# Ninety-four further index pairs in the list that edits an instruction order (hybrid attention step, one core)

## The chip, the cores and the metric

The kernel runs on one core of a Trainium2 chip, as one program. The metric is the device time of one execution in microseconds; lower is better. Where several runs are given, the median is meant.

## The reference, cut to what matters

One layer is computed for a prompt of 1024 rows and, with the same weights, for a sample group of 32 rows that also reads caches of 512 keys. Eight heads use a banded softmax attention with a relative-position bias (A), eight use stick-breaking attention (B).

```python
def in_proj(h, g_pre, w_in):
    u = rmsnorm(h, g_pre) @ w_in            # 1024 -> 4096: qa ka va ga qb kb vb gb
...
def band_attention(q, k, v, q_pos, k_pos, bias_table):
    s = jnp.einsum('bqhd,bkhd->bhqk', q, k).astype(jnp.float32) * ATTN_SCALE
    s = s + bias_table[:, rel].astype(jnp.float32)[None]
    s = jnp.where(ok[None, None], s, NEG_INF)      # own 64-frame chunk and 8 before it
    return jnp.einsum('bhqk,bkhd->bqhd', jax.nn.softmax(s, axis=-1), v)
...
def stick_breaking(q, k, v, q_pos, k_pos):
    log_beta = jax.nn.log_sigmoid(z)
    log_1m = jnp.where(causal, jax.nn.log_sigmoid(-z), 0.0)
    after = lax.cumsum(log_1m, axis=3, reverse=True) - log_1m
    w = jnp.where(causal, jnp.exp(log_beta + after), 0.0).astype(v.dtype)
...
def finish(h, oa, ga, ob, gb, w_out, g_post, p, w_ple, w_ple_gate):
    y = jnp.concatenate([oa * jax.nn.silu(ga), ob * jax.nn.silu(gb)], axis=-1) @ w_out
    h = h + rmsnorm(y, g_post)
    return h + jax.nn.sigmoid(h @ w_ple_gate) * (p @ w_ple)
```

## The kernel before, in words

**Stages.** Rows are normalised and transposed in nine tiles of 128 (`scale_x`, `turn_x`, tiles `sq`, `ptx`, `hnh`, `hnl`). The projection walks over 32 column groups of 128 (`col_steps`, accumulators `mm_qA`, `mm_kB` and so on), each in three chunks of 352 rows and 24 matmuls, since every FP32 operand is split into a high and a low half. Between them are woven the attention units: for each pair of heads and each of eight row blocks a score step (`scores`, PSUM tiles `SA`, `SB`, three banks in turn), a step that turns the weights (`weights_t`) and a value step (`values`, `PVA`, `PVB`). The later blocks of A (4 to 7) and B (4 to 6) turn their weights by way of DRAM: VectorE transposes a tile `om` in squares, a DMA stores it to `swapA` or `swapB`, and a second DMA brings it back into `be`; ScalarE then makes the high half `wTh` and VectorE the low half `wTl`. The working tiles `om`, `be`, `wTh` and `wTl` are cut from four ring buffers; a new piece waits until all readers of the old piece are done. The sample's attention loads its cached keys (`Kcs`) and values (`Vcs`) into the `be` ring. The output projection and the gate follow (o0P to g3P in the trace), with weights split and summed beforehand (`sum_dro`, `sum_drg`).

**Order.** Nothing is issued as the Python code calls it. `Recorder` collects some 9,400 operations with their dependencies, `plan` schedules them by a list of costs and due times, over and over, and `settle` then edits the winning list by hand-written pairs. `emit` issues the edited list; every engine, and SP for all DMAs, runs its share of the list in that order. A pair `(i, j)` takes the operation at place `i` and puts it at place `j`. Operations between them that it needs are taken along; the others stand behind it:

```python
for i, j in MOVES:
    x = ops[i]
    need, engines, ahead, behind = set(x.after), {x.eng}, [], []
    for o in reversed(ops[j:i]):
        if o in need or (o.eng in engines and o.eng != x.eng):
            ahead.append(o)
            need |= o.after
        ...
        else:
            behind.append(o)
    ops[j:i + 1] = ahead[::-1] + [x] + behind[::-1]
```

The pairs are applied one after the other, each to the list that the last one left, so a pair may undo part of an earlier one. All instructions stand at line 543, in `emit`; they are told apart by their tiles' names, in which buffer numbers are left out.

Of the kernel before, what the change touches and what calls it, by code (L numbers as in the profile page):

```python
# [59 lines left out]
    (6179, 6177), (4602, 4574), (5279, 5267), (1443, 1442), (847, 825), (5478, 5470), (4425, 4416), (3015, 2987), (6270, 6253), (2916, 2915),  # L60
    (2473, 2471), (5581, 5579), (6257, 6245), (5280, 5277), (4266, 4259), (240, 163), (4268, 4262), (5961, 5948), (5470, 5465), (6233, 6217),
    (4269, 4264), (4644, 4633), (1050, 1024), (4531, 4505), (2270, 2244), (1328, 1327), (4499, 4478), (2906, 2862), (1042, 997), (164, 155),
    (2916, 2915), (4633, 4620), (6698, 6684), (2245, 2244), (6511, 6457), (9153, 9149),
)
PASSES, SPREAD = 42, 400

# [1912 lines left out]
```

## Time and profile before

| | |
|---|---|
| median of three runs | 769.75 us (769.07 to 770.1) |
| time of the profiled execution | 769.5 us |
| its span, first to last instruction | 767.7 us, so 1.8 us lie around it |
| granted clock | 0.998 |
| TensorE (PE) busy | 757.9 us, 4422 matmuls |
| VectorE (DVE), ScalarE (ACT), GpSimd (POOL) busy | 589.1, 489.8, 459.7 us |
| DMA | 182.24 MB, 237 GB/s on average, all issued from SP |

Times in the trace count from the span's start. A row of the timeline gives start, duration, engine, operation, the tiles written and read, and in brackets how long the engine was idle before it and what ended that. In the view of waits, a row gives the engine that waited, for whom, the total, how many times and the longest. In the chain that ended last, a DMA's duration runs from its issue to its landing.

### The profile page before, as it was taken

Reading aid. Unit: us, or ns where it says so; the run is one execution under the profiler, and the core shown is the slowest. Engines: PE = TensorE matmul, PEld = TensorE weight load, DVE = VectorE, ACT = ScalarE, POOL = GpSimd, SP = SyncE. Lnnn points to the kernel's source line nnn. Section 1 sums busy time; section 2 is a strip of 40 time slices with the busy share of each in tenths; the row PEclk is TensorE's granted clock in tenths of the full one; section 3 lists DMA queues with packets and bytes.
Section 4 is the critical chain, followed back from the end, with each engine's and each line's share of the span. In section 5 each row is a group of like instructions: output and inputs, shape, how many; then the busy total and the mean of one; then the engine's idle time right before and its main releaser. Section 6 shows DMA issues by size and latency. Waiting matters only on the chain.

```text
span 767.7 us, 13670 instructions
## 1 busy us (share of the span) xinstructions
PE 757.9 (99%) x4422; PEld 701.4 (91%) x4422; DVE 589.1 (77%) x1025; ACT 489.8 (64%) x995; POOL 459.7 (60%) x525
## 2 busy tenths in 40 slices
PE   8999999999999999999999999999999999999997
PEld 7999999999999999999999999999998877888786
DVE  6816889898799888987898787974573578587565
ACT  6736686567685658775668685633447867774551
POOL 6614637874354546656883335787453769898443
PEclk9999999999999999999999999999999999999999
DMA  8519998878876559999779789877688859879754
GB/s 275 173 38 278 286 316 273 240 221 262 229 234 211 146 158 282 266 280 285 198 239 275 176 235 280 241 226 220 198 275 253 280 158 336 273 250 333 278 182 137
DMA packets 184825, 182.24 MB, mean 237 GB/s; under 512 B 42177, under 2 KB 139497, under 8 KB 184754
## 3 DMA queue, kind: packets, MB, share of 16 engines
q1 hardware_dynamic: 184754, 181.37, 77.6%
q8 instruction: 35, 0.57, 0.3%
q14 instruction: 36, 0.29, 0.1%
HBM read 107.62 MB, written 65.30 MB: 225 GB/s over the span
## 4 chain that ended last, share of the span: by engine, by line
PE 93%; DMA 4%; ACT 1%; DVE 1%; SPq 0%; issue 0%; ACTq 0%
PE mm_qA L543 6%; PE mm_vA L543 6%; PE mm_gB L543 6%; PE mm_kB L543 6%; PE mm_qB L543 6%; PE mm_kA L543 6%; PE mm_gA L543 5%; PE PVB L543 4%; PE mm_vB L543 4%; PE SB L543 4%; PE SA L543 4%; PE ple L543 3%; PE PVA L543 3%; PE g1P L543 3%; PE o3P L543 3%; PE o1P L543 3%
## 5 line engine op out<-in xcount | busy, mean ns | idle before, releaser
L543 POOL TENSOR_TENSOR be<-om 128x128 f32<-128x128 f32 (+7 forms) x64 | 78.0, 1224 | 55.3 <-DVE om L543 23.1
L543 DVE TENSOR_TENSOR_SCAN om<-om,SB 128x384 f32<-128x384 f32 (+5 forms) x96 | 94.4, 999 | 9.1 <-ACT om L543 8.1
L543 DVE TENSOR_TENSOR wTl<-be,wTh 128x640 fp32r<-128x640 f32 (+2 forms) x56 | 64.4, 1153 | 11.2 <-ACT wTh L543 11.1
L543 ACT ACTIVATE om<-SB 128x384 f32<-128x384 f32 (+5 forms) x96 | 44.7, 492 | 26.7 <-PE SB L543 15.1
L543 ACT CAST wTh<-be 128x640 fp32r<-128x640 f32 (+2 forms) x56 | 43.1, 774 | 19.6 <-DMA be<-swapA 12.9
L543 ACT ACTIVATE be<-om,statA 128x640 f32<-128x640 f32 (+3 forms) x64 | 46.5, 731 | 13.7 <-DVE wTl L543 6.3
L543 DVE STREAM_TRANSPOSE om<-be 128x640 f32<-128x640 f32 (+2 forms) x56 | 49.5, 890 | 4.2 <-ACT be L543 2.5
L543 POOL TENSOR_TENSOR gB<-gB,gB 128x256 f32<-128x256 f32 x32 | 25.9, 830 | 16.6 <-DMA gB<-in_w_ple_gate_dram 9.9
L543 DVE CUSTOM_DVE_ANT_0 om<-SA,biasA 128x320 f32<-128x320 f32 (+3 forms) x64 | 29.8, 483 | 7.1 <-PE SA L543 5.6
L543 ACT CAST wTh<-ptwB 128x512 fp32r<-128x512 f32 (+3 forms) x48 | 22.0, 483 | 18.6 <-PE ptwB L543 13.7
L543 PE MATMUL SB<-kdB,LB 128*128 128x384 f32 (+5 forms) x96 | 32.6, 345 | 1.1 <-DVE om L543 1.1
L543 PE MATMUL SB<-klB,LB 128*128 128x384 f32 (+5 forms) x96 | 32.9, 347 | 0.0
L543 DVE TENSOR_TENSOR wTl<-ptwB,wTh 128x512 fp32r<-128x512 f32 (+3 forms) x48 | 25.4, 542 | 6.6 <-PE PVB L543 3.9
L543 POOL TENSOR_TENSOR sggA<-sggA,oggA 128x352 f32<-128x352 f32 x24 | 26.2, 1097 | 6.1 <-DVE sggA L543 5.7
L543 PE MATMUL SA<-kdA,LA 128*128 128x320 f32 (+2 forms) x96 | 29.5, 317 | 0.1
L543 PE MATMUL SA<-klA,LA 128*128 128x320 f32 (+2 forms) x96 | 29.5, 319 | 0.0
L543 POOL TENSOR_TENSOR oB<-oB,oB 128x256 f32<-128x256 f32 x32 | 25.5, 822 | 5.0 <-DMA oB<-in_w_out_dram 5.0
L543 DVE TENSOR_TENSOR SB<-SB,maskb 128x128 f32<-128x128 f32 x64 | 18.1, 291 | 12.5 <-PE SB L543 12.1
L543 POOL TENSOR_TENSOR klB<-stkB,kdB 64x1024 fp32r<-64x1024 f32 x8 | 19.3, 2415 | 11.5 <-ACT kdB L543 10.7
L543 POOL TENSOR_TENSOR klA<-stkA,kdA 64x1024 fp32r<-64x1024 f32 x8 | 19.5, 2437 | 8.0 <-ACT kdA L543 7.8
L543 POOL TENSOR_TENSOR h<-h,x 128x512 f32<-128x512 f32 (+1 forms) x18 | 23.1, 1297 | 1.5 <-DVE h L543 1.4
L543 PE MATMUL ptwB<-ident,be 128*128 128x128 f32 x144 | 21.6, 273 | 0.0
(683 smaller groups left out, 2586.8 us busy)
## 6 DMA issues: line engine op xcount, KB each, us to landing
swapA<-om SPq DMA_DIRECT2D x32, 320.0 KB
be<-swapA SPq DMA_DIRECT2D x32, 320.0 KB
oB<-in_w_out_dram SPq DMA_DIRECT2D x16, 256.0 KB
sum_dro<-oB SPq DMA_DIRECT2D x16, 256.0 KB
gB<-in_w_ple_gate_dram SPq DMA_DIRECT2D x16, 256.0 KB
sum_drg<-gB SPq DMA_DIRECT2D x16, 256.0 KB
x<-in_x_prompt_dram SPq DMA_DIRECT2D x16, 256.0 KB
turned<-hs SPq DMA_DIRECT2D x16, 256.0 KB
```

Source lines behind the costliest of these rows:

```text
L543: getattr(getattr(tc.nc, o.what[0]), o.what[1])(*args, **kw)
```

## The change: 94 pairs more

The change appends 94 pairs to `MOVES`; nothing else differs. No operation is added or taken away, and no size, buffer or dependency changes.

```diff
-    (2916, 2915), (4633, 4620), (6698, 6684), (2245, 2244), (6511, 6457), (9153, 9149),
+    (2916, 2915), (4633, 4620), (6698, 6684), (2245, 2244), (6511, 6457), (9153, 9149), (4268, 4261), (101, 100), (1498, 1497), (102, 101), (2004, 1984),
+    (103, 102), (2526, 2512), (6051, 6050), (1200, 1144), (5579, 5557), (1051, 998), (3931, 3923), (6663, 6644), (2521, 2496), (4285, 4277),
+    (4443, 4417), (4419, 4416), (2244, 2243), (1211, 1195), (3946, 3937), (5580, 5568), (5602, 5586), (6050, 6042), (6035, 6020), (156, 155),
...
+    (6672, 6668), (3831, 3806), (2014, 1985), (6728, 6715), (6663, 6653), (2545, 2539), (2049, 2044),
```

Followed through the list, 80 operations end up ahead of something on their own engine that they stood behind: 38 DMA issues on SP, 23 operations on VectorE, 7 on ScalarE, 2 on GpSimd and 10 matmuls or transposes. Most pass one to three others. Those that the prediction speaks of, with the time at which the trace of before has them:

| at | engine | what moves | ahead of |
|---|---|---|---|
| 3.9 | PE | three of twelve `idle` matmuls, which multiply zeros | the first transpose `ptp` |
| 11.2 | POOL | the power step of `ms` (tile 0) | a cast of `wph0True` |
| 118.7 | SP | store `swapB` of a value tile | a store to `rs_dr`, a load `wr_kB` |
| 325.1 | SP | store `swapA` (block 4) | three other issues |
| 333.6 | SP | store `swapA` (block 5) | `biassA`, `wr_vA` |
| 335.6 | SP | store `swapA` (block 6) | `biassA` |
| 340.0 | SP | load `be` (block 5) | `o_dr` |
| 339.4 | DVE | a reciprocal and the mask of `SB` (block 4) | `wTl` of block 4 |
| 427.8 | DVE | two bias reductions and a cast for the sample | `sumrowA` (the first of them), `wTl` |
| 429.5 | DVE | the reduction of `SA` (block 2) | `Vl0sA` |
| 455.3 | SP | load `be` (block 7) | load `be` (block 6) |
| 461.5 | SP | one load `oggA` | six issues |
| 462.1 | SP | `Kcs` keeps its place, and a load `oggA` that stood three ahead of it comes right behind it | |
| 496.8 | SP | store `o_dr` | load `Vcs` |

The rest are moves of the same kind at other places: stores and loads of the `swap` tiles, `kt` and `vt` outputs, weight loads, bank copies and masks of the score tiles.

6 rows, old and new, of the table MOVES are left out of this document.

## The prediction

> **What bounds the kernel now.** I read the page's busy times and chain first, then the waits of PE, then busy time by stretches, and only then the timeline around each wait.
>
> ```profile
> PE 757.9 (99%) x4422; PEld 701.4 (91%) x4422; DVE 589.1 (77%) x1025; ACT 489.8 (64%) x995; POOL 459.7 (60%) x525
> ...
> PE 93%; DMA 4%; ACT 1%; DVE 1%; SPq 0%; issue 0%; ACTq 0%
> ```
>
> PE works for 757.9 of 767.7 us, and 93% of the chain that ended last is PE. No matmul is added or removed, so the change can only touch what PE spends waiting. The view of PE's waits has five rows:
>
> ```profile
> PE idle L543 <- DVE still L543: 1.3, 1, 1.3
> PE SB L543 <- DVE om L543: 1.1, 1, 1.1
> PE ptp L543 <- DMA pp<-in_p_prompt_dram: 0.9, 1, 0.9
> PE ptksB L543 <- DMA be<-in_cache_b_k_dram: 0.8, 1, 0.8
> PE PVA L543 <- ACT wTh L543: 0.5, 1, 0.5
> ```
>
> They sum to 4.6 us. Busy time by stretches says where they are (the second number behind the colon is the length, then PE busy; DMA share and GB/s stand last):
>
> ```profile
> 0.00:20.00 20.00, 17.82 (x85) 14.59 (x86) 13.18 (x20) 11.82 (x20) 13.38 (x27) 1.00 0.85 274
> 300.00:350.00 50.00, 48.44 (x308) 46.49 (x307) 43.74 (x87) 38.49 (x79) 29.99 (x41) 1.00 0.98 276
> 460.00:475.00 15.00, 14.21 (x90) 13.43 (x89) 13.93 (x23) 7.24 (x14) 8.62 (x8) 1.00 0.94 267
> 580.00:768.00 188.00, 182.52 (x802) 144.75 (x800) 123.38 (x204) 120.59 (x245) 126.96 (x121) 0.99 0.76 251
> ```
>
> At the start PE lacks 2.2 us (the waits for `still` and `pp`), between 300 and 350 us 1.6 (`SB`, `PVA`), and between 460 and 475 us 0.8 (`ptksB`). The last row lacks 5.5 us, which is the tail behind the last matmul; no move reaches it. The first matmul's wait for `still`, 1.3 us, isn't touched either. That leaves 1.1 + 0.9 + 0.8 + 0.5 = 3.3 us, and what hides in rows that count as busy.
>
> **The change part by part.** *The start.* Six of twelve `idle` matmuls run, then the first transpose of `pp` blocks PE until its load lands, and six more follow it:
>
> ```profile
> 3.84 0.45 PE L543 MATMUL ptp<-ident,pp 128*128 128x128 f32 x1 [0.88 <-DMA pp<-in_p_prompt_dram]
> 3.94 1.63 PE L543 MATMUL idle<-still 128*128 128x256 f32 x6
> 5.37 1.70 PE L543 MATMUL ptp<-ident,pp 128*128 128x128 f32 x7
> ```
>
> The six behind it take (5.37 - 3.94) / 6 = 0.24 us each. Three of them now run in the 0.88 us gap, and three times 0.24 is 0.7 us that PE no longer spends after 3.94. What is late next is the first normalised tile, which the transposes at about 12.8 us need:
>
> ```profile
> 10.62 0.61 POOL L543 CAST wph0True<-wpr_1True 128x512 fp32r<-128x512 f32 x1
> 11.21 0.56 POOL L543 TENSOR_TENSOR ms<-ms,halfp 128x1 f32<-128x1 f32 x1
> 11.80 1.41 DVE L543 SCALAR_TENSOR_TENSOR be<-om,ms,gpre 128x512 f32<-128x512 f32 x2 [1.33 <-POOL ms L543]
> 12.75 0.49 PE L543 MATMUL ptx<-ident,be 128*128 128x128 f32 x3
> ```
>
> VectorE waits 1.33 us for `ms` there. The pair that puts the power step ahead of the cast lets it begin at 10.62 and takes 0.6 us out of this chain, so the 0.7 us aren't lost to it beyond 0.1. The cast ends 0.56 us later, but its readers on GpSimd and PE come after 11.7. Term: -0.6 us; bounds 0 (the load of the next `x` or the ScalarE copies hold PE back) and -0.9 (the whole gap).
>
> A rule speaks about this stretch. Three `idle` matmuls of 256 columns take 0.72 us here, though the granted clock in the rows above is 1.00. The Trainium skill, page "TensorE: Matmul & The Clock Gate", Part 1, says the array runs at half rate until about 3.4 us of sustained work, counted in a free-running window, and that its phase varies from run to run. By it a shorter gap could open the clock a window earlier; the term would then be -0.9 instead of -0.6 (worked out among the rivals), or stay as it is.
>
> *Between 320 and 350 us.* Two waits follow each other. The chain and VectorE's timeline show them:
>
> ```profile
> 327.62 5.87 DMA gB<-in_w_ple_gate_dram
> 333.55 6.08 DMA swapA<-om
> ...
> 341.65 5.65 DMA be<-swapA
> ...
> 348.16 0.85 PE PVA L543 x4
> ```
>
> ```profile
> 338.67 0.82 DVE L543 TENSOR_TENSOR wTl<-be,wTh 128x640 fp32r<-128x640 f32 x1 [2.20 <-ACT wTh L543]
> 339.42 0.19 DVE L543 RECIPROCAL sumsA<-sumsA 128x8 f32<-128x8 f32 x1
> 339.64 0.30 DVE L543 TENSOR_TENSOR SB<-SB,maskb 128x128 f32<-128x128 f32 x1
> 339.85 1.27 DVE L543 TENSOR_TENSOR_SCAN om<-om,SB 128x512 f32<-128x512 f32 x1
> ```
>
> The scan at 339.85 frees the score bank that PE waits for at 341. The reciprocal and the mask now stand ahead of `wTl`, in the 2.20 us of idle time, so the scan starts after `wTl`, about 0.35 us earlier, and the 1.1 us become 0.7. But PE next needs the last `be` of this head: issued at 341.65, landed 5.65 us later at 347.30, and PE goes on at 348.16. What PE saves at 341 it waits longer at 348, unless that load comes sooner. Issues of SP's list are permuted ahead of it, none is removed, and it keeps its own place. The store `swapA` of block 5 moves two places up (from 333.55, where the landing of `gB` at 327.62 + 5.87 = 333.49 let it go), and with it the landing on which `be` of block 5 and a GpSimd memset depend. The last load stands behind the same number of transfers in a stretch whose DMA share is 0.98. Term: -0.1 us, near the end where nothing is gained; bounds 0 and -1.6 (both waits gone, 1.1 + 0.5). A later landing is a rival below.
>
> *At 430 us.* This one counts as busy time. The rows of VectorE and PE:
>
> ```profile
> 427.04 0.82 DVE L543 TENSOR_TENSOR wTl<-be,wTh 128x640 fp32r<-128x640 f32 x1 [2.21 <-ACT wTh L543]
> ...
> 428.90 0.69 DVE L543 TENSOR_TENSOR Vl0sA<-be,Vh0sA 128x512 fp32r<-128x512 f32 x1
> 429.51 0.55 DVE L543 CUSTOM_DVE_ANT_0 om<-SA,biasA 128x384 f32<-128x384 f32 x1
> ```
>
> ```profile
> 429.69 0.32 PE L543 MATMUL mm_qB<-hnh,wh_qB 128*128 128x352 f32 x1
> 430.12 0.42 PE L543 MATMUL SA<-kdA,LA 128*128 128x320 f32 x1
> ```
>
> The score matmul starts 0.43 us after an `mm_qB`; where 19 of those run one after the other (320.17 to 323.19 in the chain) each takes 0.16:
>
> ```profile
> 320.17 3.02 PE mm_qB L543 x19
> ```
>
> So 0.27 us are a wait for a score bank that the reduction at 429.51 frees. With the sample's reductions and cast begun in the 2.21 us of idle time, and `Vl0sA` (0.69) behind the reduction instead of ahead, the bank comes free well before 429.85. Term: -0.3 us; bounds 0 and -0.4. `wTl` ends later: the three operations now ahead of it, priced at the 0.69 of `Vl0sA` each, are 2.1 us, most of which the 2.21 us of idle time take. What is left costs nothing as long as PE is still on the score matmuls of 430.
>
> *At 469 us.*
>
> ```profile
> 455.32 5.11 DMA be<-swapA
> ...
> 462.10 6.92 DMA be<-in_cache_b_k_dram
> ```
>
> ```profile
> oggA<-rs_dr SPq DMA_DIRECT2D x24, 88.0 KB
> ```
>
> `Kcs` is issued at 462.10 and lands at 469.01, and PE waits 0.8 us for it. Its place on SP stays. One `oggA` load of 88 KB (the row above, from the DMA issues) leaves the transfers ahead of it and a small `vx` store joins them: at 267 GB/s that is 0.3 us of transfer. The load of `be` block 7, now first, lets ScalarE begin its copy up to 0.6 us (one issue) sooner, but the buffer and SP's place still hold `Kcs` at about 462. Term: -0.3; bounds 0 and -0.8.
>
> *Everything else.* The other moves lie where no row of PE's waits lies. Two of them make SP wait for data that others need not: `swapB` is moved up two places though its tile was ready for 118.74 only, and `o_dr` at 496.82 now stands ahead of `Vcs`:
>
> ```profile
> 115.57 0.56 SPq L543 DMA_DIRECT2D rs_dr<-sumrowA  x1
> ...
> 118.74 0.37 SPq L543 DMA_DIRECT2D swapB<-vxB  x1
> ...
> 492.70 0.53 SPq L543 DMA_DIRECT2D be<-in_cache_b_v_dram  x1
> 496.82 0.47 SPq L543 DMA_DIRECT2D o_dr<-otB  x1
> ...
> 515.50 0.59 DVE L543 CAST Vh0sB<-be 128x512 fp32r<-128x512 f32 x1
> ```
>
> `Vcs` is issued 4.6 us later, lands by about 497.4 + 6.9 = 504.3 with the slowest transfer above, and is read at 515.50: 11 us of cover. Behind `swapB` wait the store at 115.57 and a weight load, up to 118.74 - 115.57 = 3.2 us; neither feeds an operation that PE waits for in the five rows. I take -0.2 for all these moves together, with bounds of +0.5 and -0.5, an estimate from the largest single busy wait found above (0.27) met twice.
>
> **Sum.** -0.6 - 0.1 - 0.3 - 0.3 - 0.2 = -1.5 us against the profiled execution of 769.5 us (span 767.7 and 1.8 around it), so 768.0. The median of the three runs, 769.75, is 0.25 above the profiled one; I add nothing for it. A measurement of this kernel can tell about 0.2%, 1.5 us, from no change, so 768.2 is the border of faster and the forecast lies just below it.
>
> **Rivals.**
>
> *All waits that it reaches go* (0.16). For it: the moves crowd exactly around 322 to 340, 424 to 430 and 454 to 463 us. Against it: the last `be` and `Kcs` keep their places on SP. 769.5 - 0.9 - 1.6 - 0.3 - 0.8 = 765.9.
>
> *The clock doubles a window earlier* (0.06). Transposes at 5.37 take 1.70 / 7 = 0.24 us each, like the `idle` ones, so seven of them and three `idle` would shrink from 2.4 to 1.2 us. ScalarE's copies of the transposed tile follow them, so only some 0.3 us of the 1.2 reach the end: 768.0 - 0.3 = 767.7. The skill's clock page, named above, gives the mechanism; no run here shows it yet.
>
> *Nothing arrives* (0.20). PE's gains at the start are waited for again at 348, since the landing there doesn't move: the -0.6 of the start and the -0.1 go, and the -0.3 of 430 is waited for at 469. 769.5. For it: both places end on a DMA, and the share is 0.98 and 0.94. Against it: SP's issues hang on what PE, ScalarE and VectorE finish, so they come earlier as PE does. That pairs undo each other is a part of this rival.
>
> *A landing slips* (0.18), on the other side. Place: the last `be` at 347.30. Four transfers above take 5.11 to 6.92 us from issue to landing. If the new neighbours on the queue put it at the long end, it lands 6.92 - 5.65 = 1.3 us later, and an issue (0.56 at 115.57) that it slips behind a blocked one adds 0.6: 1.9 us. PE stands at `PVA` from the moment the load is later than the start's gain, 0.6 us, can cover. 769.5 + 1.9 - 0.3 (430) = 771.1.
>
> **How the numbers follow.** Forecast 0.40. The range reaches from the first rival to the last, 765.8 to 771.1, the bounds of the unseen moves included at the lower end; outside I leave about 2 in 10. Faster: a good half of the forecast's cases (0.27), the first two rivals (0.22) make 0.49. Same: the rest of the forecast's (0.13), the third rival (0.19) and a little of the last make 0.33. Slower: 0.18.
>
> **What would show it.** Right: the `ptp` wait falls from 0.9 to about 0.2 and `ptx` starts near 12.1; `SB <- om` falls below 0.8 while `PVA <- wTh` stays or grows; no step of 0.43 us at 430; `ptksB` waits 0.5. Wrong: the `PVA` wait is gone (then the last `be` lands early, first rival), or a new row among PE's waits of over 0.5 us, or `ptx` still at 12.7.

## The result, and the profile after

The changed kernel took 765.81 us (765.47 to 766.65) where the kernel before took 769.92 (769.07 to 770.94), four runs each: ratio 0.9946, 95% interval 0.9931 to 0.9962, 4.1 us faster. The forecast was 768.0. Two later comparisons with more runs, told below, gave 0.9972 (0.9963 to 0.9981) and 0.9966 (0.9954 to 0.9978), that is 2.2 and 2.6 us. One execution of 2641.6 us (e1 below) and one of 1057.88 us (e5), far from all others of their kernels, are in none of these ratios. The sign held and so, by 0.01 us, did the range; of the steps behind them most did not.

The changed kernel's profiled execution took 766.03 us, with a span of 764.2 us where that of before was 767.7. From its page, busy times and chain:

```profile
PE 757.5 (99%) x4422; PEld 702.8 (92%) x4422; DVE 582.2 (76%) x1025; ACT 490.2 (64%) x995; POOL 455.2 (60%) x525
...
PE 99%; DMA 1%; DVE 0%; SPq 0%; issue 0%
```

PE's busy time is the same to 0.4 us, and the chain is now 99% PE instead of 93%. Of the five rows of waits two are left:

```profile
PE idle L552 <- DVE still L552: 1.3, 1, 1.3
PE ptp L552 <- DMA pp<-in_p_prompt_dram: 0.4, 1, 0.4
```

The rows for `SB` (1.1), `ptksB` (0.8) and `PVA` (0.5) are gone. Busy time by stretches says the same (length, then PE, PEld, DVE, ACT and POOL busy):

```profile
0.00:20.00 20.00, 18.17 (x80) 14.94 (x81) 13.35 (x20) 11.99 (x20) 11.86 (x27) 1.00 0.83 271
300.00:350.00 50.00, 50.00 (x320) 48.60 (x319) 45.36 (x90) 39.15 (x79) 30.47 (x43) 1.00 0.96 282
460.00:475.00 15.00, 15.00 (x96) 14.38 (x95) 13.06 (x21) 6.57 (x12) 9.50 (x10) 1.00 0.92 267
580.00:768.00 188.00, 179.33 (x788) 142.34 (x786) 122.98 (x203) 118.46 (x241) 126.25 (x120) 0.99 0.75 247
```

PE now fills 50.00 of 50 us and 15.00 of 15. Of the 8.7 us that the last row lacks, 3.8 lie behind the end of this span, so the tail behind the last matmul is 4.9 us, where it was 5.2. For where the time went I matched each matmul with its twin in the first trace of before. The difference of their starts is PE's lag (below zero: ahead). It goes from 0 to +0.45 in the first 20 us, from +0.35 to -1.03 at 341, to -1.77 at 348, to -2.14 at 430 and to -3.15 at 469.

The first of these steps has the wrong sign. The start, in PE's timeline of the changed kernel:

```profile
3.69 0.45 PE L552 MATMUL ptp<-ident,pp 128*128 128x128 f32 x1
3.79 0.99 PE L552 MATMUL idle<-still 128*128 128x256 f32 x3
4.58 0.84 PE L552 MATMUL ptp<-ident,pp 128*128 128x128 f32 x3
5.85 1.12 PE L552 MATMUL ptp<-ident,pp 128*128 128x128 f32 x4 [0.43 <-DMA pp<-in_p_prompt_dram]
6.62 2.91 PE L552 MATMUL ple<-wph0True,php 128*128 128x512 f32 x6
...
13.49 0.60 PE L552 MATMUL ptx<-ident,be 128*128 128x128 f32 x4
```

PE is early at 4.58 and then waits 0.43 us for the second half of `pp`, a landing that the three moved `idle` matmuls had covered before, when the seven transposes ran without a gap. The six `ple` matmuls behind it take 2.91 us, about 0.43 from start to start, and the ones from 9.6 on take 0.23 to 0.24: the doubling of the matmul rate came later than in the first trace of before.

SP's issues between 333 and 342 us, before:

```profile
333.55 0.33 SPq L543 DMA_DIRECT2D swapA<-om  x1
...
335.58 1.51 SPq L543 DMA_DIRECT2D swapA<-om  x2
...
341.19 1.07 SPq L543 DMA_DIRECT2D be<-swapA  x2
```

and after:

```profile
330.76 0.58 SPq L552 DMA_DIRECT2D swapA<-om  x1
...
332.40 0.60 SPq L552 DMA_DIRECT2D swapA<-om  x1
...
333.64 0.77 SPq L552 DMA_DIRECT2D swapA<-om  x1
...
338.08 1.78 SPq L552 DMA_DIRECT2D be<-swapA  x2
```

The stores go out 2.8 to 3.2 us sooner, and the second of the two last `be` loads leaves at 339.41 instead of 341.65, although it stands at the same place of SP's list. VectorE's scan, which stood at 339.85:

```profile
336.85 0.20 DVE L552 RECIPROCAL sumsA<-sumsA 128x8 f32<-128x8 f32 x1
337.51 0.30 DVE L552 TENSOR_TENSOR SB<-SB,maskb 128x128 f32<-128x128 f32 x1 [0.45 <-PE SB L552]
337.72 1.13 DVE L552 TENSOR_TENSOR wTl<-be,wTh 128x640 fp32r<-128x640 f32 x1
338.77 1.27 DVE L552 TENSOR_TENSOR_SCAN om<-om,SB 128x512 f32<-128x512 f32 x1
```

It is 1.1 us earlier, not 0.35: the `wTl` ahead of it starts 0.95 us sooner as well. At 430 the reduction has passed `Vl0sA`, and PE's score matmul follows its `mm_qB` after 0.16 us instead of 0.43 (VectorE, then PE):

```profile
426.75 0.55 DVE L552 CUSTOM_DVE_ANT_0 om<-SA,biasA 128x384 f32<-128x384 f32 x1
...
427.23 0.68 DVE L552 TENSOR_TENSOR Vl0sA<-be,Vh0sA 128x512 fp32r<-128x512 f32 x1
```

```profile
427.93 0.33 PE L552 MATMUL mm_qB<-hnh,wh_qB 128*128 128x352 f32 x1
428.09 0.31 PE L552 MATMUL SA<-kdA,LA 128*128 128x320 f32 x1
```

`Kcs` is issued 2.3 us sooner than at 462.10, about what PE itself is early by (2.1 at 430), and yet no one waits for it:

```profile
459.79 0.52 SPq L552 DMA_DIRECT2D be<-in_cache_b_k_dram  x1
```

### The profile page after: what moved, and what is told of

It is laid out like the page before. It is cut to its first block, busy times and chain, and to the rows that moved or that the text cites. A ratio compares the mean times of both kernels' runs of the same rounds, so it can differ in the third digit from the quotient of the medians.

```text
span 764.2 us, 13673 instructions
## 1 busy us (share of the span) xinstructions
PE 757.5 (99%) x4422; PEld 702.8 (92%) x4422; DVE 582.2 (76%) x1025; ACT 490.2 (64%) x995; POOL 455.2 (60%) x525
## 4 chain that ended last, share of the span: by engine, by line
PE 99%; DMA 1%; DVE 0%; SPq 0%; issue 0%
PE mm_qA L552 6%; PE mm_kA L552 6%; PE mm_vB L552 6%; PE mm_vA L552 6%; PE mm_gA L552 6%; PE mm_gB L552 6%; PE mm_kB L552 6%; PE mm_qB L552 6%; PE SB L552 5%; PE PVB L552 4%; PE PVA L552 4%; PE SA L552 4%; PE ple L552 3%; PE g1P L552 3%; PE o3P L552 3%; PE o1P L552 3%
## 5 line engine op out<-in xcount | busy, mean ns | idle before, releaser
L552 DVE TENSOR_TENSOR wTl<-be,wTh 128x640 fp32r<-128x640 f32 (+2 forms) x56 | 60.7, 1087 | 5.3 <-ACT wTh L552 5.2
L552 POOL TENSOR_TENSOR sggB<-sggB,oggB 128x352 f32<-128x352 f32 x12 | 13.2, 1100 | 14.4 <-DVE sggB L552 14.4
```

The costliest lines, as they stand in the source:

```text
L552: getattr(getattr(tc.nc, o.what[0]), o.what[1])(*args, **kw)
```

## The experiments

Each pair list below stands behind the pairs of the kernel before; lines with a minus are taken out of the 94 of the changed kernel, and where both stand the plus lines come in their place. For one stretch the moves of one engine were written as pairs of their own that lead to the same order on that engine and leave the others as they were. Ratios are to the kernel before on the same chip, with 95% intervals; 0.001 is 0.77 us. In the table, each column is PE's lag behind the first trace of before, in us, at the time in the heading (median over some ten matmuls or more); the last three columns are absolute times: the issue of the last `be` load of this head, the start of `PVA` behind it, the first `ptx`.

| kernel | 50 | 190 | 290 | 345 | 350 | 435 | 475 | 700 | last `be` | `PVA` | `ptx` |
|---|---|---|---|---|---|---|---|---|---|---|---|
| before, first trace | 0 | 0 | 0 | 0 | 0 | 0 | 0 | 0 | 341.65 | 348.16 | 12.75 |
| before, second (e13) | 0.44 | 0.47 | 1.38 | 0.12 | -0.62 | -0.44 | -1.35 | -1.37 | 341.26 | 347.63 | 13.49 |
| before, third (e14) | -0.36 | -0.33 | 0.77 | 0.17 | -0.57 | 1.25 | 1.62 | 1.60 | 341.62 | 347.69 | 12.68 |
| start only (e1) | 0.84 | 0.84 | 0.83 | -0.09 | -0.64 | 0.38 | -0.03 | -0.05 | 341.67 | 347.52 | 13.81 |
| 424 to 470 only (e3) | 0.02 | 0.08 | 0.06 | -0.62 | -0.85 | -1.22 | -2.22 | -2.19 | 341.70 | 347.31 | 13.05 |
| 290 to 340 only (e2) | 0.60 | 0.56 | 0.86 | 0.07 | -0.39 | -0.39 | -0.70 | -0.83 | 341.36 | 347.76 | 13.61 |
| three stretches (e11) | 0.56 | 0.59 | 1.41 | 0.34 | -0.27 | -0.64 | -1.63 | -1.61 | 342.38 | 347.90 | 13.50 |
| changed, first trace | 0.45 | 0.38 | 0.35 | -1.03 | -1.77 | -2.14 | -3.15 | -3.25 | 339.41 | 346.49 | 13.49 |
| changed, second (e5) | 1.06 | 0.99 | 0.95 | 0.15 | -0.59 | -0.96 | -1.75 | -1.47 | 341.09 | 347.67 | 14.07 |
| changed, third (e15) | 0.11 | 0.04 | 0.00 | -1.14 | -1.88 | -2.24 | -3.24 | -2.97 | 339.65 | 346.38 | 12.13 |
| less idle moves (e4) | -0.09 | -0.16 | -0.19 | -1.53 | -2.27 | -2.64 | -3.17 | -3.27 | 340.36 | 345.99 | 12.66 |
| 290-340: SP's only (e6) | 0.41 | 0.34 | 0.30 | -1.06 | -1.50 | -1.84 | -2.50 | -2.61 | 341.14 | 346.65 | 12.80 |
| 290-340: not SP's (e7) | -0.66 | -0.44 | -0.47 | -1.69 | -1.19 | -1.57 | -1.93 | -2.03 | 340.39 | 346.97 | 11.80 |
| SP's last three (e9) | 0.69 | 0.62 | 0.58 | -0.62 | -1.36 | -1.74 | -2.34 | -2.44 | 340.67 | 346.90 | 12.87 |
| SP's first eight (e10) | 0.33 | 0.26 | 0.23 | -1.11 | -1.85 | -2.22 | -2.68 | -2.79 | 339.64 | 346.41 | 12.87 |
| 454-470: SP as before (e12) | 0.15 | 0.08 | 0.04 | -1.19 | -1.26 | -1.63 | -1.92 | -2.02 | 341.37 | 346.90 | 12.78 |
| start filled (e8) | -0.09 | -0.17 | -0.20 | -1.41 | -0.75 | -1.12 | -1.43 | -1.54 | 340.88 | 347.41 | 12.09 |

**The start alone.**

```diff
+    (101, 100), (102, 101), (103, 102), (156, 155),
```

> Only the four moves of the start: three idle matmuls ahead of the first transpose of pp, and the power step of ms ahead of a cast on GpSimd. Theory (a second break): the profile of the changed kernel shows PE idle again before the fifth transpose of pp (0.43 us) and its matmuls at half rate until 9.3 us instead of 7.4, 3.5 us behind that break. Then this kernel alone is slower than before by 0.3 to 0.5 us in its span, its ptx transposes start near 13.5 instead of 12.75, and PE waits for ptp about 0.4. Rival (the prediction's step): faster by 0.6, ptx near 12.1. Second rival (the moment of doubling is chance and not tied to the break): ptx anywhere between 12.1 and 13.5, the rate doubling at a time that differs from 9.3.

Ratio 1.0003 (0.9992 to 1.0015): no gain. The `ptx` transposes start at 13.81, as the theory said, and the lag at 50 us is 0.84. But three other kernels with the old start (e2, e11, e13) have `ptx` at 13.5 to 13.6 as well, so the second rival stands too.

**The changed kernel without the three idle moves.**

```diff
-    (101, 100), (102, 101), (103, 102),
```

> The changed kernel without the three pairs that move idle matmuls (91 of the 94 pairs). Theory (a second break): the start is as in the kernel before or a little better for the power step, ptx near 12.75, the rate doubles near 7.4, and the kernel is 0.3 to 0.6 us faster than the changed one: near 765.4 where the changed kernel has 765.8. Rival (the prediction's step): 0.6 us slower than the changed kernel, 766.4.

0.9966 (0.9953 to 0.9979), the same as the changed kernel later gave. The profile has `ptx` at 12.66, but the time does not tell the two starts apart.

**PE kept busy through the start.** The four transposes of the first half run together, one more `idle` matmul stands ahead of them and three behind.

```diff
+    (114, 104), (115, 105), (117, 106),
+AGAIN = [1, 1, 1, 1, 1, 1, 1, 1, 2, 1, 1, 4]
...
+                    for _ in range(again):
+                        getattr(getattr(tc.nc, o.what[0]), o.what[1])(*args, **kw)
```

> The changed kernel with PE kept busy from its first idle matmul to the second half of pp: the four transposes of the first half run together, one more idle matmul stands ahead of them and three more behind. Theory (full rate comes 3.4 to 5.7 us behind the last break): with no break behind 1.3 us the full rate comes between 4.7 and 7.0, the transposes ptx start at 11.8 to 12.8 instead of 13.5, and the kernel is 0.5 to 1.0 us faster than the changed one. Rival (chance alone): the full rate comes between 7.4 and 9.7 as everywhere, and the kernel is the same as the changed one, within 0.3. Second rival (the transfers behind it set the start): full rate early, ptx early, but the gain is waited for later, same time.

0.9971 (0.996 to 0.9982): the same as the changed kernel. The six `ple` matmuls take 1.65 us and `ptx` starts at 12.09, so the rate doubled early. But PE was not busy throughout: it still waited 0.53 us for the second half of `pp`, and the matmuls behind that wait run at the full rate at once:

```profile
6.08 0.66 PE L556 MATMUL ptp<-ident,pp 128*128 128x128 f32 x4 [0.53 <-DMA pp<-in_p_prompt_dram]
6.50 1.65 PE L556 MATMUL ple<-wph0True,php 128*128 128x512 f32 x6
```

So the early rate is not shown to come from PE having no break. What it gained was waited for again, by PE's waits of this kernel:

```profile
PE PVA L556 <- ACT wTh L556: 1.1, 1, 1.1
PE ple L556 <- ACT pleo L556: 0.8, 1, 0.8
```

The second rival fits: at 14.8 us PE stands behind ScalarE's copies `pleo`, and at 347.4 at `PVA`, where the last `be` load had been issued at 340.88.

**The stretch from 290 to 340 us alone.**

```diff
+    (4268, 4261), (3931, 3923), (4285, 4277), (4443, 4417), (4419, 4416), (3946, 3937), (4368, 4366), (4443, 4417),
...
+    (4142, 4136), (3831, 3806),
```

> Only the 22 moves between 290 and 340 us. Theory (SP runs ahead): the stores swapA of blocks 4 to 7 go out 2 to 3 us sooner, so SP no longer stands still, the last be load is issued near 339.4 though its place on SP is the same, and both waits (SB 1.1, PVA 0.5) and what follows are gone: 2.1 us less, as the step in the lag of PE between the two traces says, and the waits at 430 and 469 stay as before. Rival (the prediction's step): 0.1 us less, PVA waits 0.5 or more. Second rival (given back): 2.1 us less at 350 but more wait at 469, less than 1.5 us in all.

0.9991 (0.9981 to 1.0002), some 0.7 us. Neither row between 300 and 350 is left, but one stands later, at 0.5 instead of 0.8:

```profile
PE ptksB L546 <- DMA be<-in_cache_b_k_dram: 0.5, 1, 0.5
```

In the profiled execution PE came to 290 us with a lag of 0.86, and a PE that comes late may have less to wait for: the second profile of before, further down, came with 1.38 and has no row at `SB` or `PVA` either, without any move. The prediction's 0.1 and the theory's 2.1 were both wrong for this kernel; the second rival, less than 1.5 in all, is nearest.

**Which engine's order does it.** With SP's moves only:

```diff
-    (4443, 4417), (4419, 4416), (4368, 4366), (4394, 4393), (4380, 4367), ...
+    (3810, 3804), (3831, 3805), (3831, 3806), (3931, 3923), (3946, 3937), (4142, 4136), (4234, 4202), (4268, 4263), (4285, 4271), (4345, 4286), (4430, 4421),
```

> The changed kernel, but between 290 and 340 us only SP's list is that of the changed kernel (11 moves); VectorE and TensorE run in the order of before there. Theory (SP's list carries it, since the last be load leaves SP 2.2 us sooner): the wait at PVA stays gone, the wait at SB (VectorE's reciprocal and mask behind the weights) is 0 to 0.4; at most 0.4 us slower than the changed kernel. Rival (the prediction's reading: VectorE's order takes 0.35 off the SB wait, SP's list nothing): SB waits 1.1 and PVA 0.2 or more, 1.5 us slower or more.

0.9974 (0.9964 to 0.9985), no row at `SB` or `PVA`: as the changed kernel, within the interval. And the reverse:

```diff
+    (4284, 4283), (4368, 4366), (4380, 4367), (4417, 4416), (4442, 4417), (4394, 4393),
```

> The reverse: between 290 and 340 us VectorE and TensorE run in the order of the changed kernel (6 moves), SP's list is that of before. Theory (SP's list carries it): the SB wait comes back with 0.7 to 1.1 and PVA with 0.3 to 0.8, 1.3 to 2.0 us slower than the changed kernel, the last be load issued 2 us later than in the changed kernel. Rival (VectorE's and TensorE's order carries it): within 0.4 of the changed kernel.

0.9995 (0.9983 to 1.0007): against the changed kernel on this chip (e5, 0.9972) 1.8 us of the gain are gone by the ratios, 1.5 by the means of the runs, give or take 0.9. The theory said 1.3 to 2.0. The waits differ from it: `SB` has no row, and `PVA` has the longest one.

```profile
PE PVA L551 <- ACT wTh L551: 1.0, 1, 1.0
```

This row lies at 346.97. No wait at 341 and one at `PVA` instead is what the prediction's mechanism gives for VectorE's order alone. This one profile doesn't show it: PE came early to this stretch (-0.47), so a part of the row is that lead; e8, with all of SP's moves, has a row of 1.1 at the same place; and the last `be` load was issued at 340.39, sooner than in any profile of before, though SP's list is that of before.

**Which of SP's moves.** Only the last three, `swapA` of blocks 5 and 6 and `be` of block 5:

```diff
+    (4285, 4271), (4345, 4286), (4430, 4421),
```

> The changed kernel, but of the 11 moves of SP's list between 290 and 340 us only the last three: swapA of blocks 5 and 6 ahead of loads, and be of block 5 ahead of a store. Theory (the stores that the be loads follow are what SP's list held back): as the changed kernel within 0.5, the last be load issued near 339.5, no PVA wait. Rival (the eight earlier moves, 290 to 330, let SP run ahead by 1 us before the stores come): PVA waits 0.4 or more, 0.5 to 1.5 us slower than the changed kernel.

0.9989 (0.9977 to 1.0001). Only the first eight, of which three move `swapA` stores of blocks 4 and 5 up, one the store of `sumrowA`, and the others loads:

```diff
+    (3810, 3804), (3831, 3805), (3831, 3806), (3931, 3923), (3946, 3937), (4142, 4136), (4234, 4202), (4268, 4263),
```

> The reverse of the run with three: of SP's 11 moves between 290 and 340 us only the first eight. Theory (the stores): the last be load is issued near 341, PVA waits 0.5 or more, 1.0 to 1.8 us slower than the changed kernel. Rival (the eight earlier moves): as the changed kernel within 0.5.

0.9969 (0.9957 to 0.998). In both profiles the waits at `SB` and `PVA` are gone. The eight early moves are enough; with the last three alone the kernel is some 1.5 us slower than that, though the two intervals just touch and e10 has five runs only. My theory, that it is the late stores, falls. What the eight do is seen in SP's timeline of e10:

```profile
325.25 2.09 SPq L552 DMA_DIRECT2D gB<-in_w_ple_gate_dram  x2
...
331.95 0.45 SPq L552 DMA_DIRECT2D swapA<-om  x1
```

The `swapA` of block 5 goes out at 331.95 instead of 333.55, though this store keeps its old place. In e7, without SP's moves, the same store goes at 332.65, although PE came to 290 us 0.7 us earlier there than in e10.

**From 424 to 470 us alone.**

```diff
+    (6051, 6050), (5579, 5557), (5580, 5568), (5602, 5586), (6050, 6042), (6035, 6020), (6043, 6007), (6051, 6043),
...
+    (6045, 6034), (5996, 5990), (5541, 5530), (6007, 5991),
```

> Only the 19 moves between 424 and 470 us. Theory: the steps of the traces hold alone, 0.4 at 430 and 1.0 at 469, together 1.4 us less; ptksB no longer waits. Rival (the prediction's terms): 0.3 and 0.3, together 0.6, ptksB still waits 0.5. Second rival (it needs the earlier time from 320 to 350): nothing at 469, 0.4 in all.

0.9992 (0.998 to 1.0005). In the profile the steps are there in full, 0.37 at 430 and 1.0 at 469, and `ptksB` has no row; the measured gain, some 0.6 us, can't tell 1.4 from 0.6. The step of 1.0 counts from the first trace of before, which waited 0.8 there; the second, without any move, shows 0.9 between 435 and 475 us as well.

**SP's list from 454 to 470 us as before.**

```diff
-    (6051, 6050), (6050, 6042), (6035, 6020), (6043, 6007), (6051, 6043), (5960, 5959), ...
+    (6039, 6028),
```

> The changed kernel, but between 454 and 470 us SP's list is that of before (VectorE's one move stays). Theory (SP's list carries the step at 469 too): ptksB waits 0.5 to 1.0 for Kcs, up to 1.0 us slower than the changed kernel. Rival (Kcs comes sooner because of what went before, 300 to 430): no row for ptksB, same time.

0.9972 (0.9961 to 0.9983), no row for `ptksB`: the rival fits. SP's moves there show no gain of their own when the other moves stand.

**The three stretches together, without the other 53 pairs.**

> The kernel before with the 41 moves of the three stretches (290 to 340, 424 to 430, 454 to 470 us) and none of the other 53. Theory (these three carry all of it): as the changed kernel, 2.0 to 2.6 us faster than before, and no row over 0.4 among PE's waits behind the start. Rival (the other 53 moves carry part: the prediction had -0.2 for them and -0.6 for the start): 0.5 us or more slower than the changed kernel. Where the single stretches together gave less, 0.7 and 0.6, than the whole: if waits stand one behind the other, so that one that is taken away is waited for at the next, the three together give more than that sum.

0.9977 (0.9964 to 0.999), 1.8 us. Most of the gain, and the interval leaves open whether all. The trace says not quite: between 190 and 285 us, where none of these 41 moves lies, PE loses 0.8 us in this execution (lag 0.59 to 1.41), and half of it is a row of PE's timeline:

```profile
205.69 0.86 PE L548 MATMUL PVA<-wTh,v2A 128*128 128x512 f32 x4 [0.44 <-ACT wTh L548]
```

More on this stretch below.

**The changed kernel and the kernel before, again.**

> The changed kernel itself once more, as the measure for the three below. In the six profiles so far the matmuls of the start reach their full rate at 7.4, 7.9, 8.5 and 9.5 us where the idle matmuls stand as before (one break of PE, ending at 3.8) and at 9.6 and 9.7 where three are moved (a second break, ending at 5.9 to 6.2). Theory (second break): again 9.4 or later here, as the full rate comes 3.5 to 5.7 us behind the last break. Rival (chance alone): any time from 7.4 to 9.7. In the time: 765.5 to 766.7, with no row of PE's waits from 300 to 475 us of over 0.4.

0.9972 (0.9963 to 0.9981). The theory on the second break would have held by this profile alone (`ptx` at 14.07), but e6 and e7, with the same start, have `ptx` at 12.80 and 11.80. It falls; the last section has the times of the full rate.

> The kernel before, profiled once more. If the waits of the first profile (SB 1.1, PVA 0.5, ptksB 0.8, the step at 430) belong to this order, the same rows stand here within 0.3. If they are one draw of how the transfers land, other rows stand here, with a sum of 1.5 to 3.5 us behind the start, and the span differs from 767.7 by up to 1.5.

> The kernel before a third time, for the same question: the same rows of waits within 0.3, or other rows with a sum of 1.5 to 3.5 us.

768.15 and 771.11 us. These are PE's waits in the second profile of before:

```profile
PE idle L543 <- DVE still L543: 1.3, 1, 1.3
PE ptp L543 <- DMA pp<-in_p_prompt_dram: 0.7, 1, 0.7
PE SA L543 <- DVE statA L543: 0.3, 1, 0.3
```

and in the third:

```profile
PE mm_qB L543 <- ACT stqB L543: 1.3, 1, 1.3
PE ptksB L543 <- DMA be<-in_cache_b_k_dram: 1.2, 1, 1.2
PE ptp L543 <- DMA pp<-in_p_prompt_dram: 0.7, 1, 0.7
PE SB L543 <- DVE om L543: 0.4, 1, 0.4
PE SA L543 <- DVE statA L543: 0.4, 1, 0.4
```

The same program, three sets of rows. `SB` waits 1.1, nothing, 0.4; `ptksB` 0.8, nothing, 1.2; a row of 1.3 for `mm_qB` stands in the third alone. Behind the start the rows sum to 2.4, 0.3 and 3.3 us; the 0.3 is less than either text expected. The rows behind the start on which the prediction's sum was built are one draw.

> The changed kernel a third time. If its gain is 4.1 us, as in the four runs of the first comparison, the ratio comes to 0.9946 or so; if it is the 2.2 of the second, to 0.9972. In its profile no row of PE's waits between 20 and 580 us of over 0.4, and a lag at the start that depends on when the full rate begins.

0.9966 (0.9954 to 0.9978), 2.6 us, and the interval leaves 0.9946 out. Its profile has no row between 20 and 580 us:

```profile
PE idle L552 <- DVE still L552: 1.3, 1, 1.3
PE ple L552 <- ACT pleo L552: 0.9, 1, 0.9
PE ptp L552 <- DMA pp<-in_p_prompt_dram: 0.2, 1, 0.2
```

## Why the prediction was right or wrong

The first rival, that all waits which the moves reach go, gave 765.9, and the kernel took 765.8 in the first comparison. Its number was met by luck: it counted 0.9 us from the start, where PE lost 0.45, and 1.6, 0.3 and 0.8 at the other three places, where PE gained 2.1, 0.4 and 1.0. Of the prediction's own signs for being wrong two came: the `PVA` wait was gone, and `ptx` came no earlier than 12.7. Over the 115 runs of before in the five comparisons the median is 769.0, over 27 of the changed kernel 766.8. So 2.2 to 2.6 us is the better measure of the gain; that the first four runs of each were a poor draw for before and a good one for the changed kernel is the likely reason, not a tried one. The forecast's -1.75 is thus nearer than the first comparison says, but not by its own steps.

*Start, -0.6: wrong, sign and reason.* "What is late next" was named as `ms`; it is the second half of `pp`, which released PE at 5.85 us and which the same `idle` matmuls had hidden. Half of the gap came back there (0.88 became 0.10 and 0.43). What else the start takes is the moment at which the rate doubles, and that differs between executions of one order. Over the nine profiles with the three moves the lag at 50 us is 0.38 on average (-0.66 to 1.06), over the seven without 0.17 (-0.36 to 0.60); e8 is left out. A gain of 0.6 doesn't show; the changed kernel without the three moved matmuls (e4) takes the same time within the intervals.

*320 to 350, -0.1: this is the step that failed, and the wrong reason is "it keeps its own place".* The prediction took the unchanged place of the last `be` load for an unchanged time, so that what PE saves at 341 it would wait for at 348. In the first pair of traces the load left 2.2 us sooner, both waits were gone, and the step was 2.1 us. In the runs SP's order carries it: without SP's moves 1.5 to 1.8 us of the gain are missing (e7), without VectorE's and PE's nothing that can be measured (e6), and the stretch alone gives 0.7 (e2). How SP's order does it stays open. In the five profiles without any move between 290 and 340 us the last `be` load is issued between 341.26 and 341.70, though PE came to 290 us with a lag anywhere from 0 to 1.38. With SP's moves there, all or a part of them, in the otherwise changed kernel it goes at 339.4 to 341.4, and `PVA` starts at 346.0 to 347.7 instead of 347.3 to 348.2. But e2 and e11, with SP's moves, have 341.4 and 342.4, and e7, without them, 340.4, so this load is not shown to be the carrier. That SP runs ahead because fewer of its issues stand still is read from the rows at 333 to 337; it was not tried by itself.

*430, -0.3: right for the first trace.* Between 350 and 435 us PE gains 0.34 to 0.38 in each of the twelve profiles that have the moves. What the prediction couldn't see is that this place costs more in other executions of before: between 350 and 435 us the lag grows by 0.2 in the second trace, by 1.8 in the third and by 1.0 in e1, ahead of `mm_qB` and `SA`. No profile with the moves has such a row.

*469, -0.3: 1.0 in the first pair of traces; the cause stays open.* `Kcs` did keep its place and was issued hardly sooner against PE, as forecast, but it landed in time. None of the twelve profiles with moves at 424 to 470 us has a row for `ptksB`, e12 among them, where SP's list there is that of before; of the five others three have one (0.8, 1.2, 0.5). How much of it is the transfers that share the queues, no run told apart.

*Everything else, -0.2: small in the first pair of traces (about -0.2, and 0.3 less tail, which the prediction had as out of reach), larger on average.* From 190 to 290 us PE loses 0.9 and 1.1 us, against the first trace, in the second and third trace of before, 0.8 in e11 and 0.3 in e2, and nothing in two; in none of the ten profiles with the other moves does it lose anything. The first page of before had nothing to show there. Which of those pairs does it was not tried.

*The error under the steps* was to take the rows of one execution as the price of the order. The kernel before pays at one place in one execution and at another in the next: three profiles, spans of 766.4, 767.7 and 769.3. Why was not traced; landings that vary are one candidate (the second half of `pp` released PE anywhere between 5.52 and 6.22 us in nine profiles), but the row of 1.3 for `mm_qB` names ScalarE. The changed order gains the mean of these waits, not the sum of one page's rows; in the first trace they happened to be 2.4 us in rows and 3.5 in the lag.

The table (and for the tail the spans) gives these means: in each stretch, how much PE's lag grows on average in the profiles with the moves of that stretch and in those without. The difference is +0.2 us in the first 50 (nine profiles with, seven without), -0.5 from 50 to 290 (ten, seven), -0.5 from 290 to 350 (eleven with SP's moves, five without any), -1.0 from 350 to 435 (twelve, five), -0.5 from 435 to 475 (eleven without e12, five) and -0.2 behind that, tail included. Together that is about -2.4 before rounding, the gain that the later comparisons measured. With five to seven profiles without the moves each difference is good to some 0.4 to 0.7 us only, but the order of the sizes is another than on the first page: the place at 430, which had no row there, comes out largest. Such a mean also fits that one stretch alone gives little (0.7 and 0.6); that what it saves is waited for again at the next stretch is possible too, and not shown.

Three readings in the prediction are off by little: the rival of the slipping landing counts four transfers where its rows show five; the 5.5 us of the last stretch are a tail of 5.2 and 0.3 behind the span's end; and the chances of forecast and rivals, whose times all lie inside the range, add up to 1, which leaves nothing for the 2 in 10 outside.

No version here beats the changed kernel: e4, e6, e8, e10 and e12 are equal to it within their intervals.

## What to carry to other kernels

Before pricing waits of about a microsecond, look at two or three profiles of the same kernel: rows that come and go are the spread of one order's executions, and a change of order is worth their mean. A place in a queue is not a time: ask what holds the queue up ahead of it. And before moving filler work into one wait, ask which later landing the filler covered where it stood.

## What the runs showed of the hardware

The time at which matmuls reach their full rate is not set by the order alone. The six `ple` matmuls of the start in the changed kernel's second and third profile, as in the first at 2.91 us:

```profile
6.98 2.91 PE L552 MATMUL ple<-wph0True,php 128*128 128x512 f32 x6
```

```profile
6.29 1.92 PE L552 MATMUL ple<-wph0True,php 128*128 128x512 f32 x6
```

Over all profiles the group takes 1.65 to 2.91 us, and the first `ptx` starts between 11.80 and 14.07. The granted clock of 1.00 in the rows of this stretch is no sign of the full rate: the clock record kept in the trace begins, at 1.00, only at 7.35, 9.13 and 7.50 us in the three profiles of before and at 9.46, 10.21 and 6.89 in those of the changed kernel, where the matmuls' steps halve, and the view counts the time ahead of its first entry as full. Over all profiles the record begins between 4.72 (e7) and 10.21 (e5). In e7, e8, e9 and e12 it begins before PE's wait for the second half of `pp` ends (at 5.58 to 6.20), and that wait of 0.40 to 0.90 us did not take the rate back.

The Trainium skill, page "TensorE: Matmul & The Clock Gate", Part 1, says that the window behind this runs freely, that the change moves by about 500 ns from run to run, and that a model should not be fitted to one count. The kind of behaviour agrees; the spread here is larger, some 2 us for one order (`ptx` at 12.13 to 14.07), and the prediction's -0.6 was worked out from one execution.

Only a part of an early start lasts here: in the six profiles with `ptx` before 12.9 and the moved start PE then waits 0.3 to 0.9 us for ScalarE's `pleo` copies. They have `ptx` 1.25 us sooner on average than the other three with that start, and a lag at 50 us that is 0.6 lower.
